# Hybrid decoder step: the per-layer embedding projection is placed among the last down slabs, and the final stage uses the pools of the second feed-forward block

## The chip, the cores and the metric

The kernel runs on one core of one Trainium2 chip. Its metric is the time of one execution in device microseconds (us). A core has TensorE (PE; loads of its stationary operand are listed apart as PEld), VectorE (DVE), ScalarE (ACT), GpSimd (POOL) and a queue engine (SP) that issues nearly all transfers. Each engine works through its own list of instructions in order; semaphores make one wait for another.

## The reference, cut to what matters

One layer on 544 tokens (512 of a new sequence, 8 times 4 of running ones), width 1024:

```python
x = x + 0.5 * _swiglu(_rmsnorm(x, n_f1), w_f1u, w_f1d)
m, ... = _mixer(_rmsnorm(x, n_mix), ...)               # SSD heads and HGRN2 heads
x = x + m
x = x + 0.5 * _swiglu(_rmsnorm(x, n_f2), w_f2u, w_f2d) # d_ff 2816
gate = sigmoid(_rmsnorm(x, n_ple) @ w_ple_gate)        # 1024 x 1024
e = _rmsnorm(p @ w_ple_proj, ple_post)                 # p: 544 x 256
x = x + gate * e
y = _rmsnorm(x, norm_final)
```

What matters here: `e` depends on the input `p` alone, not on `x`; `gate` needs the finished `x`.

## The kernel before

Everything is kept transposed: a tile is 128 features (partitions) by 544 tokens, and `x` is eight such tiles, `xs[0]` to `xs[7]`, parts of one buffer `xb`. fp32 products are made of three fp32r products: every operand is split into a high part (a rounded copy, made on ACT) and a low part (the rest, made on DVE), and hi·hi, hi·lo and lo·hi are summed in PSUM. `mm6` (line 229) is that for one 128x128 weight block and one tile: six matmuls of 272 columns. `slab` (line 133) loads eight weight blocks into a raw buffer `wraw`, of which there are two, and splits them into `whi` and `wlo`, of which there are three each. The PSUM pool `big` has two buffers; the down slabs, the embedding projection and the first gate products share it.

The stages around the change, in order:

- The second feed-forward block, `ffn` (line 235), with pool `f2`. Its up part runs in 18 periods in an order that is written out by hand (`pin` ties the instructions of each engine into a chain). The last group of six hidden tiles is multiplied by the down weights at its end: eight slabs, one for each `m`, 36 matmuls each, and after each one DVE adds the sum to `xs[m]` (line 643, in the trace `xb` at L72). There the chain is off (`pinned[0] = False`), and the framework's scheduler sets the order of each engine.
- The final stage, pool `f3` (line 1246). It loads `p` (`pt`), splits it into `pth` and `ptl`, and computes `e` in eight groups (PSUM `ps_e`, 12 matmuls each, copied to SBUF by ACT at line 1269). `rms_split` splits the scaled `x` (`xwh` on ACT, `xwl` on DVE), and `rms_two` squares `x` on ACT and sums the squares into two accumulators, one on POOL and one on DVE. `gslab` loads and splits the gate weights (`gh`, `gl`). The gate products follow in two halves of 272 tokens, eight groups of 24 matmuls in each (PSUM `ps_pg` and `ps_s`, line 1344).
- A root mean square is made by `inv_rms2` (line 179): each accumulator is multiplied by a column of ones in five one-column products (PSUM `ps_s`; each is two passes in the trace), the root and the reciprocal are taken, and the result is spread by products with the identity. It is done for `x` (result `r`) and for `e` (`eacc`, which then scales the eight `e` tiles on DVE).

Of the kernel before, what the change touches and what calls it, by code (L numbers as in the profile page):

```python
# [9 lines left out]
F32 = mybir.dt.float32  # L10
# [7 lines left out]
P = 128  # L18
T = 544
# [29 lines left out]
def body(ctx, tc, xT, pT, hconv, hssm, hhg, vecs, csts, w1u, w1d, w_in, w_dt, w_o, w2u, w2d, w_pg, w_pp,  # L49
# [21 lines left out]
    def stt(out, a, s, b, op0, op1):  # L71
        pin(V.scalar_tensor_tensor(out=out, in0=a, scalar=s, in1=b, op0=op0, op1=op1))  # L72
# [161 lines left out]

    def ffn(xs, nname, wu, wd, fp, ht, acc=None, load=None, side=iter(())):
        pinned[0] = True
# [403 lines left out]
        for m in range(KD):  # L640
            t = ts_[m] if m < 2 else last_slab(m)
            part(t, range(n - 1, n) if m < 2 else range(n))
            stt(h2(xs[m]), t[0][:, :, :HN], 0.5, h2(xs[m]), ALU.mult, ALU.add)

    x_sp = dram.tile([KD, P, T], F32, name="x_sp")
# [94 lines left out]
    with tc.tile_pool(name="ma", bufs=20, reuse_waits="tile") as ap:  # L740
# [499 lines left out]

        with tc.tile_pool(name="f2", bufs=1, reuse_waits="tile") as fp:
            ffn(xs, "n_f2", w2u, w2d, fp, ring, acc2, side=ssm_updates(
                fp, ring, lambda: xp2.tile([P, 512], F32R, name="xst", tag="sqa", bufs=1)))


    with tc.tile_pool(name="f3", bufs=34, reuse_waits="tile") as fp:
        def hslot(nm, dt=F32):
            return fp.tile([P, T], dt, name=nm, tag="h")

        def eslot(nm, dt=F32):  # L1250
            return fp.tile([P, T], dt, name=nm, tag="e", bufs=12)

        ph, es = [], []
        wpp = [slab(w_pp[i]) for i in range(2)]
        for k in range(2):
            t = eslot("pt")
            nc.sync.dma_start(t, pT[k])
            hi, lo = eslot("pth", F32R), eslot("ptl", F32R)
            A.copy(hi, t)
            tt(lo, t, f32(hi), ALU.subtract)  # L1260
            ph.append((hi, lo))
        for m in range(KD):
            hi, lo = wpp[m // 4]
            ps = big.tile([P, 2, 512], F32, name="ps_e", tag="big")
            for k in range(2):
                i = 2 * (m % 4) + k
                mm6(ps, hi[:, i], lo[:, i], ph[k][0], ph[k][1], k == 0, k == 1)
            e = eslot("e")
            A.copy(h2(e), ps[:, :, :HN])
            es.append(e)  # L1270
        xw = rms_split(xs, "n_ple")
        acc_x = rms_two(xs, fp)
        eacc = fp.tile([P, T], F32, name="eacc", bufs=1)

        def e_scale():
            ea = rms_two(es, fp)
            yield
            inv_rms(eacc, ea, 1024)
            for m in range(KD):
                stt(es[m], es[m], vc("ple_post", m), eacc, ALU.mult, ALU.mult)  # L1280
            yield

        eg = e_scale()
        wg = []

        def gslab(m):
            hi = [hslot("gh", F32R) for _ in range(2)]
            lo = [hslot("gl", F32R) for _ in range(2)]
            raw = wp.tile([P, 8, P], F32, name="wraw", tag="wraw", bufs=2)
            nc.sync.dma_start(raw, w_pg[m])  # L1290
            for i in range(2):
                rv = raw[:, 4 * i:4 * i + 4].rearrange("p a b -> p (a b)")
                A.copy(hi[i][:, :512], rv)
                tt(lo[i][:, :512], rv, f32(hi[i][:, :512]), ALU.subtract)
            wg.append((hi, lo))

        gslab(0)
        gslab(1)

        def final(hf, acc, sq):  # L1300
# [4 lines left out]
            for c, o in enumerate(cks):  # L1305
                PE.matmul(pq[:, c:c + 1], acc[:, o:o + P], ones[:, 0:1], start=True, stop=True)
            ra = fp.tile([P, 8], F32, name="ra", bufs=2)
            V.tensor_copy(ra[:, 0:3], pq[:, 0:3])
# [6 lines left out]
            for c, o in enumerate(cks):  # L1315
                a = 2 * P - o if c == 2 else 0
                PE.matmul(pr[:, o + a:o + P], ra[:, c:c + 1].to_broadcast([P, P]), cs("ident")[:, a:], start=True,
                          stop=True)
            rs = hslot("rs")[:, :HN]
            A.copy(rs, pr[:, :HN])  # L1320
# [10 lines left out]
        for hf in range(2):  # L1331
# [3 lines left out]
            for m in range(KD):  # L1335
# [10 lines left out]
                if hf == 0 and m == 1:  # L1346
                    r = rms_r(acc_x)
                if hf == 0 and m in (2, 4):
# [6 lines left out]
                for i, ps in pend:  # L1355
                    t = fp.tile([P, HN], F32, name="gt", tag="ft", bufs=4)
                    tt(t, ps[:, :HN], r[:, sl], ALU.mult)
                    act(t, t, AF.Sigmoid)
                    if hf == 1 and i == KD - 1:
                        tc.keep_in_program_order(A.preload_act_table(AF.Sqrt))  # L1360
                    tt(t, t, es[i][:, sl], ALU.mult)
                    tt(xs[i][:, sl], xs[i][:, sl], t, ALU.add)
                    sq = xqa[:, sl] if i == 0 else fp.tile([P, HN], F32, name="xq", tag="xq", bufs=2)
                    act(sq, xs[i][:, sl], AF.Square)
                    act(xs[i][:, sl], xs[i][:, sl], AF.Copy, scale=vc("n_fin", i))
                    if acc is None:
                        acc = sq
                    elif i < KD - 1:
                        tt(acc, acc, sq, ALU.add)
                pend = []  # L1370
            fin = final(hf, acc, sq)
        for _ in fin:
            pass


# [98 lines left out]
```

## Time and profile before

| | |
|---|---|
| median of 3 runs | 1417.15 us (1417.12 to 1419.89) |
| the profiled execution | 1418.97 us, of which the span of the engines is 1417.2 us |
| TensorE busy | 1384.7 us, 98% of the span |
| VectorE / ScalarE / GpSimd busy | 1000.6 / 684.3 / 268.8 us |
| mean granted TensorE clock | 0.984 of full speed |
| TensorE in the chain that ended last | 92% |

A row of the timeline gives the start, the duration, the engine, the line, the operation with output and inputs, a count, and in brackets how long the engine had sat idle and for whom. A matmul of 272 columns is listed at some 288 ns, but matmuls overlap, so that the next begins 125 ns later; a busy TensorE can still be one at half its clock, and the column PEclk of a stretch tells which. The last 94 us of the span, after the last down slab, are the final stage.

### The profile page before, as it was taken

Reading aid. Unit: us, or ns where it says so; the run is one execution under the profiler, and the core shown is the slowest. Engines: PE = TensorE matmul, PEld = TensorE weight load, DVE = VectorE, ACT = ScalarE, POOL = GpSimd, SP = SyncE. Lnnn points to the kernel's source line nnn. Section 1 sums busy time; section 2 is a strip of 40 time slices with the busy share of each in tenths; the row PEclk is TensorE's granted clock in tenths of the full one; section 3 lists DMA queues with packets and bytes.
Section 4 is the critical chain, followed back from the end, with each engine's and each line's share of the span. In section 5 each row is a group of like instructions: output and inputs, shape, how many; then the busy total and the mean of one; then the engine's idle time right before and its main releaser. Section 6 shows DMA issues by size and latency. Waiting matters only on the chain.

```text
span 1417.2 us, 27123 instructions
## 1 busy us (share of the span) xinstructions
PE 1384.7 (98%) x11069; PEld 1342.9 (95%) x11069; DVE 1000.6 (71%) x1603; ACT 684.3 (48%) x1232; POOL 268.8 (19%) x245
## 2 busy tenths in 40 slices
PE   7999999999999999999999999999899999999997
PEld 7999999999999999999999799999899999999896
DVE  6696666666568887777776577566877777776465
ACT  6544444443444365555553375455444444443655
POOL 0133332232111100000001021101333333320200
PEclk9999999999999999999999999999999999999898
DMA  6133233332432422222222445551344443334311
GB/s 228 43 93 105 90 90 94 100 95 73 149 111 77 139 93 93 93 93 93 93 100 72 140 152 172 187 170 46 107 120 125 128 137 120 119 101 116 105 45 64
DMA packets 67901, 154.99 MB, mean 109 GB/s; under 512 B 8576, under 2 KB 15872, under 8 KB 67776
## 3 DMA queue, kind: packets, MB, share of 16 engines
q1 hardware_dynamic: 66192, 150.65, 33.7%
q10 hardware_dynamic: 1584, 2.61, 0.5%
q8 instruction: 87, 1.43, 0.4%
q14 instruction: 38, 0.31, 0.1%
HBM read 138.70 MB, written 14.52 MB: 108 GB/s over the span
## 4 chain that ended last, share of the span: by engine, by line
PE 92%; DVE 4%; ACT 2%; issue 1%; DMA 0%; SPq 0%; DVEq 0%; ACTq 0%
PE ps_in L84 22%; PE ps_s L84 19%; PE ps_dn L84 19%; PE ps_ed L84 10%; PE ps_wo L84 6%; PE ps_up L84 4%; PE ps_s L1344 3%; PE ps_e L84 1%; PE ps_s L946 1%; PE ps_s L943 1%; PE ps_pg L1344 1%; DVE wlo L69 1%; DVE raw L69 1%; ACT whi L81 1%; PE ps_s L1056 1%
## 5 line engine op out<-in xcount | busy, mean ns | idle before, releaser
L81 ACT CAST whi<-wraw 128x1024 fp32r<-128x1024 f32 (+2 forms) x140 | 132.2, 950 | 200.5 <-PE ps_in L84 88.8
L69 DVE TENSOR_TENSOR wlo<-wraw,whi 128x1024 fp32r<-128x1024 f32 (+2 forms) x140 | 156.9, 1125 | 82.5 <-ACT whi L81 78.5
L84 PE MATMUL ps_in<-xwh,whi 128*128 128x272 f32 x832 | 183.6, 297 | 0.0
L84 PE MATMUL ps_in<-xwh,wlo 128*128 128x272 f32 x832 | 175.5, 291 | 0.0
L84 PE MATMUL ps_in<-xwl,whi 128*128 128x272 f32 x832 | 173.6, 289 | 0.0
L84 PEld LDWEIGHTS ps_in<-xwh,whi 128*128 128x128 f32 x832 | 132.4, 188 | 8.5 <-issue 8.2
L81 ACT COPY s<-ps_s 128x272 f32<-128x272 f32 x108 | 41.5, 384 | 195.5 <-PE ps_s L84 195.5
L84 PEld LDWEIGHTS ps_in<-xwh,wlo 128*128 128x128 f32 x832 | 130.7, 189 | 2.9 <-issue 2.9
L84 PEld LDWEIGHTS ps_in<-xwl,whi 128*128 128x128 f32 x832 | 131.1, 189 | 1.5 <-issue 1.5
L84 PE MATMUL ps_dn<-hl,dh 128*128 128x272 f32 x512 | 106.0, 288 | 2.5 <-DVE hl L69 2.5
L84 PE MATMUL ps_dn<-hh,dh 128*128 128x272 f32 x512 | 106.2, 289 | 0.0
L84 PE MATMUL ps_dn<-hh,dl 128*128 128x272 f32 x512 | 105.8, 288 | 0.0
L69 POOL TENSOR_TENSOR wraw<-r,r 128x512 f32<-128x512 f32 x36 | 48.7, 1353 | 263.4 <-DVE r L69 263.4
L84 PE MATMUL ps_s<-bx,w3h 128*128 128x272 f32 x576 | 85.2, 291 | 3.5 <-ACT s L81 3.5
L84 PEld LDWEIGHTS ps_dn<-hl,dh 128*128 128x128 f32 x512 | 80.5, 188 | 3.0 <-DVE hl L69 3.0
L84 PEld LDWEIGHTS ps_s<-bx,w3h 128*128 128x128 f32 x576 | 77.6, 191 | 3.9 <-ACT s L81 3.9
L84 PEld LDWEIGHTS ps_dn<-hh,dl 128*128 128x128 f32 x512 | 80.3, 188 | 0.2 <-DVE dl L69 0.2
L84 PEld LDWEIGHTS ps_dn<-hh,dh 128*128 128x128 f32 x512 | 80.4, 189 | 0.0
L69 POOL TENSOR_TENSOR g<-g,r 128x544 f32<-128x544 f32 x36 | 64.7, 1797 | 57.3 <-ACT g L89 56.0
L89 ACT ACT_TABLE_LOAD x55 | 70.6, 1283 | 4.4 <-DVE g L69 3.2
L69 DVE TENSOR_TENSOR w3l<-r,w3h 128x1024 fp32r<-128x1024 f32 x38 | 46.8, 1230 | 34.7 <-ACT w3h L81 34.7
L69 POOL TENSOR_TENSOR r<-r,wraw 128x512 f32<-128x512 f32 x36 | 49.2, 1366 | 103.4 <-DMA wraw<-in_w2u 54.8
(385 smaller groups left out, 3579.0 us busy)
## 6 DMA issues: line engine op xcount, KB each, us to landing
wraw<-in_w_in SPq DMA_DIRECT2D x52, 512.0 KB, 3.3
r<-in_w1u SPq DMA_DIRECT2D x22, 512.0 KB, 4.6
r<-in_w2u SPq DMA_DIRECT2D x22, 512.0 KB, 4.8
dr<-in_w1d SPq DMA_DIRECT2D x32, 256.0 KB, 3.3
h<-in_hssm SPq DMA_DIRECT2D x32, 256.0 KB, 4.1
wraw<-in_w_o SPq DMA_DIRECT2D x16, 512.0 KB, 4.2
dr<-in_w2d SPq DMA_DIRECT2D x32, 256.0 KB, 3.6
r<-in_w1u SPq DMA_DIRECT2D x18, 256.0 KB, 3.1
```

The source lines that it names most:

```text
L69: pin((eng or V).tensor_tensor(out=out, in0=a, in1=b, op=op))
L81: pin(A.copy(out, a))
L84: pin(PE.matmul(out, w, x, **kw))
L89: ins = pin(A.activation(out=out, in_=in_, func=f, scale=scale, bias=bias, **kw))
L943: PE.matmul(py[64 * e:64 * e + 64, q * P:q * P + n], xdt[:n, 2 * q + e], E[:n, 2 * q + e, :n], start=True, stop=pi is None, tile_position= ...
L946: PE.matmul(py[:, q * P:q * P + n], yf[:, q * P:(q + 1) * P], cs("sel") if smpl else cs("ident"), start=False, stop=True)
L1056: PE.matmul(pat[32 * j:32 * j + 32, c * P:(c + 1) * P], cw[:, c * P + 32 * j:c * P + 32 * j + 32], qs, start=True, stop=True, tile_positio ...
L1344: PE.matmul(ps[:, :HN], w[k // 4][:, k % 4 * P:k % 4 * P + P], xw[k][x][:, sl], start=k == 0 and n == 0, stop=k == KD - 1 and n == 2)
```

## The change

`ffn` gets an argument `done_m`, a function that it calls after each of the eight last down slabs. The final stage no longer opens a pool of its own. In the function `after_m` that is handed over, slab by slab:

- after every slab, `xs[m]` is split (`xwh`, `xwl`) and squared, and the square is added on DVE to one accumulator (`sqa`) instead of two;
- after slab 2, `p` is loaded and split and the first half of the projection weights is loaded; after slab 3, four of the eight `e` groups are computed; after slabs 5 and 6 the second half and the gate slabs 0 and 1 are loaded; after slab 6 come two `e` groups, after slab 7 the last two. Each `e` tile is squared and summed on DVE into one accumulator (`ea`).

The tiles take slots of the feed-forward block: `xw2`, `g`, `s53`, `s12`, `r1` to `r3`, `w3h`, `w3l`, `w5h`, `w5l`, `dh`, `dl`, and the ring of 544-wide tiles. The diff, without the lines that only rename a slot in the gate loop:

```diff
@@ -232,7 +232,7 @@
                 mm(ps, (lo if n == 2 else hi)[:, o + k], (xl if n == 1 else xh)[:, k % 2],
                    start=start and k == 0 and n == 0, stop=k == 3 and n == 2, skip_group_check=not start)
 
-    def ffn(xs, nname, wu, wd, fp, ht, acc=None, load=None, side=iter(())):
+    def ffn(xs, nname, wu, wd, fp, ht, acc=None, load=None, side=iter(()), done_m=None):
         pinned[0] = True
         chain.clear()
         X = {}
@@ -641,6 +641,8 @@
             t = ts_[m] if m < 2 else last_slab(m)
             part(t, range(n - 1, n) if m < 2 else range(n))
             stt(h2(xs[m]), t[0][:, :, :HN], 0.5, h2(xs[m]), ALU.mult, ALU.add)
+            if done_m:
+                done_m(m)
 
     x_sp = dram.tile([KD, P, T], F32, name="x_sp")
     acs_d = dram.tile([5, 16, P], F32, name="acs_d")
@@ -1238,64 +1240,95 @@
             acc2 = rms_sq(xs, xp2, 6, tmp=xp)
 
 
-        with tc.tile_pool(name="f2", bufs=1, reuse_waits="tile") as fp:
-            ffn(xs, "n_f2", w2u, w2d, fp, ring, acc2, side=ssm_updates(
-                fp, ring, lambda: xp2.tile([P, 512], F32R, name="xst", tag="sqa", bufs=1)))
-
-
-    with tc.tile_pool(name="f3", bufs=34, reuse_waits="tile") as fp:
-        def hslot(nm, dt=F32):
-            return fp.tile([P, T], dt, name=nm, tag="h")
-
-        def eslot(nm, dt=F32):
-            return fp.tile([P, T], dt, name=nm, tag="e", bufs=12)
-
-        ph, es = [], []
-        wpp = [slab(w_pp[i]) for i in range(2)]
-        for k in range(2):
-            t = eslot("pt")
-            nc.sync.dma_start(t, pT[k])
-            hi, lo = eslot("pth", F32R), eslot("ptl", F32R)
-            A.copy(hi, t)
-            tt(lo, t, f32(hi), ALU.subtract)
-            ph.append((hi, lo))
-        for m in range(KD):
-            hi, lo = wpp[m // 4]
-            ps = big.tile([P, 2, 512], F32, name="ps_e", tag="big")
+        end = ExitStack()
+        fp = end.enter_context(tc.tile_pool(name="f2", bufs=1, reuse_waits="tile"))
+
+        def et(nm, dt=F32):
+            return fp.tile([P, T], dt, name=nm, tag="xw2", bufs=12)
+
+        def ft(tag, nm, bufs, dt=F32):
+            return fp.tile([P, T], dt, name=nm, tag=tag, bufs=bufs)
+
+        ph, es, xw, ea, wpp = [], [], [], {}, []
+
+        def square(key, src, tags, home):
+            if key not in ea:
+                ea[key] = home()
+                act(ea[key], src, AF.Square)
+            else:
+                sq = ft(*tags)
+                act(sq, src, AF.Square)
+                tt(ea[key], ea[key], sq, ALU.add)
+
+        def e_load():
             for k in range(2):
-                i = 2 * (m % 4) + k
-                mm6(ps, hi[:, i], lo[:, i], ph[k][0], ph[k][1], k == 0, k == 1)
-            e = eslot("e")
-            A.copy(h2(e), ps[:, :, :HN])
-            es.append(e)
-        xw = rms_split(xs, "n_ple")
-        acc_x = rms_two(xs, fp)
-        eacc = fp.tile([P, T], F32, name="eacc", bufs=1)
+                t = ring("pt")
+                nc.sync.dma_start(t, pT[k])
+                hi, lo = et("pth", F32R), et("ptl", F32R)
+                A.copy(hi, t)
+                tt(lo, t, f32(hi), ALU.subtract)
+                ph.append((hi, lo))
+
+        def e_part(ms):
+            for m in ms:
+                hi, lo = wpp[m // 4]
+                ps = big.tile([P, 2, 512], F32, name="ps_e", tag="big")
+                for k in range(2):
+                    i = 2 * (m % 4) + k
+                    mm6(ps, hi[:, i], lo[:, i], ph[k][0], ph[k][1], k == 0, k == 1)
+                e = et("e")
+                A.copy(h2(e), ps[:, :, :HN])
+                es.append(e)
+                square("e", e, ("s53", "esq", 2), lambda: ft("s12", "ea", 1))
+
+        def after_m(m):
+            xw.append(split(xs[m], vc("n_ple", m)))
+            square("x", xs[m], ("g", "sq", 2), lambda: xp2.tile([P, T], F32, name="sqa", tag="sqa", bufs=1))
+            if m == 2:
+                e_load()
+                wpp.append(slab(w_pp[0]))
+            elif m == 3:
+                e_part(range(4))
+            elif m == 5:
+                wpp.append(slab(w_pp[1]))
+                gslab(0)
+            elif m == 6:
+                e_part((4, 5))
+                gslab(1)
+            elif m == 7:
+                e_part((6, 7))
 
         def e_scale():
-            ea = rms_two(es, fp)
             yield
-            inv_rms(eacc, ea, 1024)
+            eacc = ft("g", "eacc", 2)
+            inv_rms(eacc, [ea["e"]], 1024)
             for m in range(KD):
                 stt(es[m], es[m], vc("ple_post", m), eacc, ALU.mult, ALU.mult)
             yield
 
-        eg = e_scale()
         wg = []
 
         def gslab(m):
-            hi = [hslot("gh", F32R) for _ in range(2)]
-            lo = [hslot("gl", F32R) for _ in range(2)]
+            if m in (0, 4, 5, 6, 7):
+                hi, lo = ([ring(n, F32R)[:, :512] for _ in range(2)] for n in ("gh", "gl"))
+            else:
+                f = lambda n, w: fp.tile([P, w, P], F32R, name="gw", tag=n, bufs=1).rearrange("p a b -> p (a b)")
+                if m == 3:
+                    hi, lo = f("r3", 8), (f("w5h", 4), f("w5l", 4))
+                else:
+                    hi, lo = [f(n, 8) for n in (("w3h", "w3l") if m == 1 else ("r1", "r2"))]
+                hi, lo = [t if isinstance(t, tuple) else (t[:, :512], t[:, 512:]) for t in (hi, lo)]
             raw = wp.tile([P, 8, P], F32, name="wraw", tag="wraw", bufs=2)
             nc.sync.dma_start(raw, w_pg[m])
             for i in range(2):
                 rv = raw[:, 4 * i:4 * i + 4].rearrange("p a b -> p (a b)")
-                A.copy(hi[i][:, :512], rv)
-                tt(lo[i][:, :512], rv, f32(hi[i][:, :512]), ALU.subtract)
+                A.copy(hi[i], rv)
+                tt(lo[i], rv, f32(hi[i]), ALU.subtract)
             wg.append((hi, lo))
 
-        gslab(0)
-        gslab(1)
+        ffn(xs, "n_f2", w2u, w2d, fp, ring, acc2, side=ssm_updates(
+            fp, ring, lambda: xp2.tile([P, 512], F32R, name="xst", tag="sqa", bufs=1)), done_m=after_m)
+        eg = e_scale()
 
         def final(hf, acc, sq):
             sl = slice(hf * HN, (hf + 1) * HN)
...
                 if hf == 0 and m == 1:
-                    r = rms_r(acc_x)
+                    r = rms_r([ea["x"]])
```

The order of ScalarE's instructions, where the down slabs end and `p` is cast. Before, from the split of `xs[6]` on:

```order
L89 ACTIVATE xwh_15724<-xb_9826,vec_67 128x544
L89 ACTIVATE sq_15732<-xb_9826 128x544
L89 ACTIVATE sq_15734<-xb_9826 128x544
L89 ACTIVATE xwh_15728<-xb_9826,vec_67 128x544
L89 ACTIVATE sq_15737<-xb_9826 128x544
L89 ACTIVATE sq_15740<-xb_9826 128x544
L1259 CAST pth_15570<-pt_15568 128x544
```

Now, at the second of the eight down slabs (`hh_15232` is the last hidden tile, `whi_15301` and `whi_15370` are the weights of down slabs 2 and 3, `whi_15364` the projection weights):

```order
L81 CAST whi_15301<-wraw_15300 128x768
L81 CAST hh_15232<-g_15172 128x544
L1268 CAST pth_15353<-pt_15351 128x544
L81 CAST whi_15364<-wraw_15363 128x1024
L1268 CAST pth_15359<-pt_15357 128x544
L81 CAST whi_15370<-wraw_15369 128x768
L89 ACTIVATE xwh_15280<-xb_9826,vec_67 128x544
```

The first cast of `p` has moved from behind the split of the last `xs[m]` and two squares to a place ahead of the third down slab.

VectorE at the same place. Before, after the last state update (`h0_15175`); `ps_dn_15157` and `ps_dn_15217` are the sums of down slabs 0 and 1, whose PSUM buffers the slabs 2 and 3 take over:

```order
L69 TENSOR_TENSOR h0_15175<-h0_15175,ps_s_15269 128x512
L72 SCALAR_TENSOR_TENSOR xb_9826<-ps_dn_15157,xb_9826 128x544
L69 TENSOR_TENSOR wlo_15333<-wraw_15331,whi_15332 128x768
L72 SCALAR_TENSOR_TENSOR xb_9826<-ps_dn_15217,xb_9826 128x544
L69 TENSOR_TENSOR wlo_15377<-wraw_15375,whi_15376 128x768
```

Now, up to the low part of the weights of down slab 3 (`wlo_15371`; before it was `wlo_15333`):

```order
L69 TENSOR_TENSOR h0_15175<-h0_15175,ps_s_15269 128x512
L69 TENSOR_TENSOR ptl_15354<-pt_15351,pth_15353 128x544
L72 SCALAR_TENSOR_TENSOR xb_9826<-ps_dn_15157,xb_9826 128x544
L72 SCALAR_TENSOR_TENSOR xb_9826<-ps_dn_15217,xb_9826 128x544
L69 TENSOR_TENSOR ptl_15360<-pt_15357,pth_15359 128x544
L69 TENSOR_TENSOR wlo_15365<-wraw_15363,whi_15364 128x1024
L72 SCALAR_TENSOR_TENSOR xwl_15281<-xb_9826,vec_67,xwh_15280 128x544
L69 TENSOR_TENSOR sqa_15284<-sqa_15284,sq_15297 128x544
L72 SCALAR_TENSOR_TENSOR xwl_15294<-xb_9826,vec_67,xwh_15293 128x544
L69 TENSOR_TENSOR wlo_15371<-wraw_15369,whi_15370 128x768
```

One instruction now stands ahead of the first `xb`, and six of the final stage stand ahead of the low part of slab 3's weights.

VectorE later, around down slab 6 (`ps_dn_15615`); `gw_15697` and `gw_15861` are the low parts of gate slabs 1 and 2, `wlo_15706` that of down slab 7:

```order
L69 TENSOR_TENSOR gw_15697<-wraw_15698,gw_15696 128x512 x2
L72 SCALAR_TENSOR_TENSOR xb_9826<-ps_dn_15548,xb_9826 128x544
L72 SCALAR_TENSOR_TENSOR xwl_15587<-xb_9826,vec_67,xwh_15586 128x544
L69 TENSOR_TENSOR sqa_15284<-sqa_15284,sq_15590 128x544
L69 TENSOR_TENSOR wlo_15706<-wraw_15704,whi_15705 128x768
L69 TENSOR_TENSOR gw_15861<-wraw_15862,gw_15860 128x512
L72 SCALAR_TENSOR_TENSOR xb_9826<-ps_dn_15615,xb_9826 128x544
L69 TENSOR_TENSOR gw_15861<-wraw_15862,gw_15860 128x512
L72 SCALAR_TENSOR_TENSOR xwl_15654<-xb_9826,vec_67,xwh_15653 128x544
```

The addition of down slab 6 to `xb`, which frees the PSUM buffer of the sixth `e` group, stands behind the first half of gate slab 2, and so behind that slab's transfer.

## Rows read from the trace of the kernel before

**Rows 1.** Chain of waits, 1290 to 1350 us: start, duration, what.
```profile
1295.53 27.25 PE ps_dn L84 x216
...
1322.80 0.74 DVE xb L72
...
1325.31 0.64 ACT pth L1259
...
1346.86 3.25 PE ps_pg L1344 x26
```

**Rows 2.** Instructions on tile ps_e: min/median/max ns, first and last start.
```profile
L84 PE MATMUL ps_e<-pth,whi x32: 285/288/593, 1326.0 to 1346.1; 128*128 128x272 f32 x32
```

**Rows 3.** Timeline of TensorE, rows from the whole span.
```profile
400.51 1.20 PE L84 MATMUL ps_s<-cst,ra 128*128 128x128 f32 x10
...
829.02 1.17 PE L84 MATMUL ps_s<-ones,ysq 128*128 128x1 f32 x10
...
842.25 1.28 PE L84 MATMUL ps_s<-ones,ysq 128*128 128x1 f32 x10 [0.78 <-DVE ysq L69]
...
1325.99 1.05 PE L84 MATMUL ps_e<-pth,whi 128*128 128x272 f32 x3 [3.23 <-ACT pth L1259]
...
1352.70 0.75 PE L84 MATMUL ps_s<-cst,ra 128*128 128x128 f32 x6
...
1362.37 2.29 PE L84 MATMUL ps_s<-ones,sq 128*128 128x1 f32 x20
...
1365.24 1.94 PE L84 MATMUL ps_s<-cst,ra 128*128 128x128 f32 x10 [0.58 <-DVE ra L180]
```

**Rows 4.** Stretches: length, busy PE, PEld, DVE, ACT, POOL, PEclk, DMA share, GB/s.
```profile
829.00:830.00 1.00, 1.00 (x12) 1.00 (x10) 1.00 (x3) 0.98 (x3) 0.00 (x0) 1.00 0.06 16
...
844.00:845.00 1.00, 1.00 (x6) 1.00 (x6) 1.00 (x2) 0.99 (x5) 0.00 (x0) 0.50 0.56 158
...
1290.00:1322.00 32.00, 31.93 (x255) 31.67 (x255) 20.29 (x27) 13.32 (x18) 1.01 (x1) 1.00 0.37 116
...
1326.00:1338.20 12.20, 12.20 (x53) 11.91 (x54) 6.59 (x9) 7.52 (x13) 2.05 (x2) 0.50 0.14 44
...
1368.00:1369.00 1.00, 1.00 (x7) 1.00 (x6) 1.00 (x2) 0.00 (x0) 0.00 (x0) 0.50 0.00 0
```

**Rows 5.** Timeline of VectorE, 1294 to 1377 us.
```profile
1295.41 0.96 DVE L69 TENSOR_TENSOR wlo<-wraw,whi 128x768 fp32r<-128x768 f32 x1
1296.29 0.72 DVE L72 SCALAR_TENSOR_TENSOR xb<-ps_dn,xb 128x544 f32<-128x544 f32 x1
...
1297.79 1.48 DVE L72 SCALAR_TENSOR_TENSOR xwl<-xb,vec,xwh 128x544 fp32r<-128x544 f32 x2
...
1314.69 1.23 DVE L69 TENSOR_TENSOR wlo<-wraw,whi 128x1024 fp32r<-128x1024 f32 x1 [0.15 <-ACT whi L81]
...
1330.89 0.72 DVE L69 TENSOR_TENSOR ptl<-pt,pth 128x544 fp32r<-128x544 f32 x1
...
1367.65 5.66 DVE L72 SCALAR_TENSOR_TENSOR e<-e,vec,eacc 128x544 f32<-128x544 f32 x8 [2.47 <-ACT eacc L81]
...
1376.40 0.43 DVE L69 TENSOR_TENSOR gt<-ps_s,r 128x272 f32<-128x272 f32 x1
```

**Rows 6.** Timeline of the weight loads where down slab 2 begins.
```profile
1295.53 0.30 PEld L84 LDWEIGHTS ps_dn<-hh,whi 128*128 128x128 f32 x2 [0.29 <-DVE xb L72]
```

**Rows 7.** Instructions that write or read sq: min/median/max ns.
```profile
L69 DVE TENSOR_TENSOR sq<-sq x17: 718/725/1656, 24.8 to 1348.5; 128x544 f32<-128x544 f32 x17
...
L69 POOL TENSOR_TENSOR sq<-sq x14: 1341/1366/2182, 369.0 to 1345.6; 128x544 f32<-128x544 f32 x14
```

**Rows 8.** Transfers of the last 150 us, and of in_w_pg.
```profile
wraw<-in_w2d SPq DMA_DIRECT2D x8, 384.0 KB, 3.4
...
DMA to landing us min/median/max: 3.1/3.2/4.4
```

**Rows 9.** Instructions on tile wraw, 1300 to 1365 us: min/median/max ns.
```profile
L1293 ACT CAST gh<-wraw x16: 603/616/622, 1328.0 to 1361.7; 128x512 fp32r<-128x512 f32 x16
```

More of the change, by code (lines that the diff above doesn't have):

```diff
@@ L1306, in final @@
                 PE.matmul(pq[:, c:c + 1], acc[:, o:o + P], ones[:, 0:1], start=True, stop=True)
-            ra = fp.tile([P, 8], F32, name="ra", bufs=2)
+            ra = wp.tile([P, 8], F32, name="ra", tag="ra", bufs=2)
             V.tensor_copy(ra[:, 0:3], pq[:, 0:3])
@@ L1318, in final @@
                           stop=True)
-            rs = hslot("rs")[:, :HN]
+            rs = ft("g", "rs", 2)[:, :HN]
             A.copy(rs, pr[:, :HN])
@@ L1355, in body @@
                 for i, ps in pend:
-                    t = fp.tile([P, HN], F32, name="gt", tag="ft", bufs=4)
+                    t = fp.tile([P, 4, P], F32, name="gt", tag=("dh", "dl")[i % 2], bufs=2).rearrange("p a b -> p (a b)")[:, :HN]
                     tt(t, ps[:, :HN], r[:, sl], ALU.mult)
@@ L1362, in body @@
                     tt(xs[i][:, sl], xs[i][:, sl], t, ALU.add)
-                    sq = xqa[:, sl] if i == 0 else fp.tile([P, HN], F32, name="xq", tag="xq", bufs=2)
+                    sq = xqa[:, sl] if i == 0 else ft("s53", "xq", 2)[:, :HN]
                     act(sq, xs[i][:, sl], AF.Square)
@@ L1373, in body @@
             pass
+        end.close()
 _INS = ["xT", "pT", "hconv", "hssm", "hhg", "vecs", "csts", "w1u", "w1d", "w_in", "w_dt", "w_o", "w2u",
```

## The prediction

> **What bounds the kernel now.** The page's table of busy engines came first: TensorE is busy for 98% of the span and stands for 92% of the chain of waits. So the time is the sum of the matmuls, unless TensorE waits or runs at less than its full clock, and I looked for those places from the last down slabs on, where the diff begins. The chain of waits shows the seam [rows 1]: 216 down matmuls run without a break from 1295.53 to 1322.78 us, then the chain leaves TensorE for DVE and ACT until `p` is cast, and the gate products begin only at 1346.86. TensorE's own timeline gives the wait: 3.23 us for the first `pth` [rows 3]. The stretches give the rest: from 1326.0 to 1338.2 TensorE is busy all the time but at a granted clock of 0.50, 1.2 GHz, while it had 1.00, 2.4 GHz, up to 1322 [rows 4]. What it did before the fall was to wait, and what it did in the slow stretch was partly 20 one-column passes for the mean square of `x`. There is a second such stretch, still at 0.50 at 1368, after the 20 one-column passes for `e` and a wait of 0.58 us [rows 3, 4]. The list of DMA waits held nothing for TensorE here.
>
> **The change part by part.** Up to down slab 1 all engines have the same order; the terms begin there.
>
> 1. *The seam goes.* From 1322.78 to 1346.86 are 24.08 us [rows 1]. The work in it at full clock: 96 matmuls on `ps_e` (three forms of 32 [rows 2]), at 27.25 / 216 = 0.126 us each [rows 1], 12.1 us; 20 one-column passes, 2.29 us; four passes of 128 columns at 0.75 / 6 us, 0.5 us [rows 3]. That is 14.9 us, so 9.2 us were lost: 3.2 us of waiting, the rest half clock. In the changed order `p` is cast before down slab 2, the last two `e` groups (24 matmuls, 3.0 us) stand behind down slab 7, and the last `xb` and the split of `xs[7]` (0.72 and 0.78 us on DVE [rows 5], and one pass of ACT over a tile of that size, as for `pth`, 0.64 [rows 1]) are done beside them, and the gate products come to `xs[7]` last. What is late next is then the psum copy of the `e` groups (term 3). Gain 9.2 us; its lower bound is the 3.2 us of waiting alone, should the slow clock stay for another reason.
>
> 2. *One accumulator instead of two.* Both mean squares take 10 one-column passes instead of 20. Twenty took 2.29 us, ten took 1.17 us [rows 3]: 1.1 us each, 2.2 us. The 14 additions that this puts on DVE, eight of them more than before (six went to POOL), are 0.72 us each where POOL is quiet [rows 7], 10.1 us beside some 40 us of matmuls, in which DVE was busy 20.3 of 32 us [rows 4]: hidden, but queued ahead of things TensorE waits for (term 3). If that cover were gone, 5.8 us at most would come back. On these additions the Trainium skill (SBUF — State Buffer, Who interferes with whom) says that a DVE instruction with two inputs in SBUF shuts out a GpSimd instruction that reads SBUF, and the reverse. The trace agrees: the same addition took 725 ns as a rule and up to 1656 where POOL added too [rows 7]. With POOL idle the sum has 0.72 us for each; by 1.66 us it would have 0.9 us more in the wait for slab 3's weights.
>
> 3. *New waits in the down slabs.* Slab 2 takes over the PSUM buffer of slab 0, and TensorE already waits 0.29 us for DVE's `xb` there [rows 6]. One `ptl` (0.72 us, 0.64 to the next start [rows 5]) now stands ahead of it: 0.6 us more, slab 2 begins at 1296.1. Its 36 matmuls end at 1296.1 + 36 x 0.126 = 1300.6, and slab 3 needs its low weights after four more, at 1301.1. On DVE, from the first `xb` on, stand `xb` 0.72, `ptl` 0.72, `wlo` of the projection 1.23, `xwl` 0.78, an addition 0.72, `xwl` 0.78 and that `wlo` 0.96 [rows 5, 7]; less 0.08 us of overlap at each step (eight of 0.78 take 5.66 [rows 5]) it is done at 1301.4: 0.3 us of waiting. Before down slab 7 TensorE needs the PSUM buffer of the fifth `e` group, whose copy stands on ACT behind a split and a square of `xs[6]`: it is ready about when the sixth group ends, 0 to 0.4 us, and I take 0.4. The sixth `e` group needs `xb` of slab 6, which stands behind half of gate slab 2. That slab's load is issued about when slab 5 ends (T); landing 3.2 us [rows 8], cast 0.62 [rows 9], low half 0.96 x 512 / 768 = 0.64 [rows 5], issue and steps between some 0.4: T + 4.9, then `xb` to T + 5.6, needed at T + 36 x 0.126 + 12 x 0.126 = T + 6.0. So nothing, with 0.4 us to spare. Sum 1.3 us lost; the bounds are 0.3 us and, with all these transfers at the 4.4 us that one gate slab took [rows 8], 4 us.
>
> 4. *The second slow stretch* stays in the forecast. Ten passes (1.17 us) and a wait of some 0.6 us for root and reciprocal remain. The row nearest to that is at 842: a wait of 0.78 us and ten passes, after which the clock fell to 0.50 at 844; ten passes at 829 without a wait left it at 1.00 [rows 3, 4]. Cost of the change 0; if it goes, up to 1.8 us are gained (the ten passes of 128 columns took 1.94 instead of 1.20 us [rows 3], and some 2 us of matmuls until 1369 took twice their time [rows 4]). About 0.65 us of that would turn into a wait, since DVE frees the next PSUM buffer only at 1376.83 [rows 5], 9.65 us after the last of those passes, and three gate groups at full clock take 9.0 us.
>
> The loads, casts and splits of the gate weights keep their number; they are made earlier, on queues that had room (ACT busy 13.3 of 32 us [rows 4]), and cost nothing unless they come late. Nothing changes in the last half of the gate or in the end.
>
> Sum: 9.2 + 2.2 - 1.3 = 10.1 us. The profiled execution took 1418.97 us (span 1417.2 us and 1.8 us around it), so it would take 1408.9 us; it lies 1.8 us above the median of the runs, 1417.15 us, from which I get 1407.1 us.
>
> **The rivals.**
>
> *The second fall goes too.* For it: half the passes, and the ones at 829 had no fall. Against it: the wait behind them stays, as at 842. It gives 1.2 us more: 1405.9 us.
>
> *Small waits add up and the clock falls in the down slabs.* If transfers land later than 3.2 us, the sixth `e` group waits (1.2 us if gate slab 2 alone takes 4.4 us), other waits grow, and TensorE works in short groups with pauses. One fall costs about 1.8 us, as in term 4. For it: the two raw buffers now carry three streams through one SP queue, and each load waits for DVE. Against it: the clock stayed at 1.00 with the 0.29 us wait [rows 4, 6]. Waits of 4 instead of 1.3 us, and one fall: 10.1 - 2.7 - 1.8 = 5.6 us of gain, 1411.5 us. The Trainium skill has a rule on the side of this rival (TensorE: Matmul & The Clock Gate, A second HAM failure mode: psum-queue depth-cycling): a TensorE that pauses briefly between groups as it goes round its PSUM banks can swing between its two clocks. The wait of 0.29 us, with the clock at 1.00 after it, does not bear it out; the fall at 844, after 0.78 us and the one-column passes, can be read its way.
>
> *Slower: the two raw buffers become the bound.* Between slab 2's weights and the start of slab 7, ten loads pass through the two `wraw` buffers, five each. A round is landing 3.4, a cast 0.62 x 768 / 512 = 0.93 and a low part 0.96 us [rows 5, 8, 9], 5.3 us; five rounds are 26.5 us, and end at 1322.6 even if they begin only with slab 2, at 1296.1. TensorE starts slab 7 at about 1296.1 + 5 x 4.54 + 6 x 1.51 = 1328. So each round may take 6.4 us before slab 7 is late at all, and at 8.8 us slab 7 is 12 us late and the time 2 us above before, 1419. For it: every load waits for a DVE instruction that stands in order behind others. Against it: the longest landing in the rows is 4.4 us, and DVE had 12 of 32 us free.
>
> *It doesn't do what it says.* If TensorE still met `pth` or the first projection weights late, or lost at the gate what it gains at the seam, the time stays at about 1417. The order on ACT speaks against it: the cast of `p` waits there for its transfer alone, with ACT idle.
>
> **How the numbers follow.** Forecast 1407.1 us: 0.47. Second fall gone: 0.25, 1405.9. Small waits and a fall: 0.20, 1409 to 1414. No change: 0.05. Slower: 0.03. The range goes from the sum with the second fall gone and the lower bound of the waits (10.1 + 1.2 + 1.0 = 12.3 us, 1404.8) to just beyond the price of the third case, 1412.0; what it leaves out is a part of the third case and the last two. A measurement of this kernel tells about 0.2% (2.8 us) from no change: faster by more, below 1414.3 us, 0.93; within it 0.04; slower 0.03.
>
> **What the changed profile would show.** Right: no wait of TensorE for `pth`; a granted clock of 1.00 from 1300 to the gate products, which begin near 1336; ones products in groups of ten passes; waits of `ps_dn` for `xb` under 1 us and for `wlo` of about 0.3 us; the `e` stretch near 1355 with a fall behind it. Wrong: a wait of over 1 us inside the down slabs with PEclk 0.50 behind it, TensorE waiting for a transfer of `w2d` or `w_pg`, or gate products that begin later than 1340.

## The result and the profile after

The changed kernel takes 1408.07 us (median of 6 runs, 1405.26 to 1411.82), the kernel before 1417.13 us (6 runs, 1413.29 to 1419.89): a ratio of 0.9939, 95% interval 0.9922 to 0.9956. A second series of 5 runs gave 1408.17 us, ratio 0.9932 (0.9918 to 0.9945). The forecast was 1407.1 us.

The profiled execution of the changed kernel took 1406.71 us, its span is 1404.9 us, against 1418.97 and 1417.2. Of these 12.3 us, 2.75 lie ahead of the change. The last state product on TensorE, up to which all engines have the same order, begins earlier by that (start, duration, then engine, line and operation; before first):

```profile
1293.57 0.39 PE L84 MATMUL ps_s<-xst,Bm 128*128 128x512 f32 x1
```

```profile
1290.82 0.39 PE L84 MATMUL ps_s<-xst,Bm 128*128 128x512 f32 x1
```

The last section says more on that. What the change does is counted from this product on: 9.6 us less (123.63 and 114.08 us to the end), where the sum in the prediction was 10.1; between the medians it is 9.1 us.

First the chain of waits of the changed kernel from slab 2 to the gate products, start, duration and what; it answers to [rows 1]:

```profile
1293.27 5.26 PE ps_dn L84 x40
1298.56 4.28 PE ps_dn L84 x32
1302.83 4.54 PE ps_e L84 x36
...
1313.06 4.67 DMA wraw<-in_w_pg
1317.75 0.63 ACT gw L1325
1318.41 1.31 DVE gw L69 x2
1319.73 3.12 DMA wraw<-in_w_pg
1322.87 0.63 ACT gw L1325
1323.53 0.69 DVE gw L69
1324.22 0.65 DVE xb L72
...
1326.74 4.78 PE ps_dn L84 x36
1331.52 3.02 PE ps_e L84 x24
1334.54 6.00 PE ps_pg L1377 x48
```

The seam is gone: the gate products begin at 1334.54, 41.3 us after slab 2 begins (51.3 before). The six slabs and eight `e` groups in between are 27.25 + 12.1 = 39.3 us, so 1.9 us of waiting are left. For one part of it the chain leaves TensorE and follows two transfers of gate weights. TensorE's own timeline has these waits, and those at `e` [rows 3 and 6 show them before]:

```profile
1293.27 0.52 PE L84 MATMUL ps_dn<-hh,whi 128*128 128x272 f32 x2 [0.55 <-DVE xb L72]
...
1324.91 0.52 PE L84 MATMUL ps_e<-pth,whi 128*128 128x272 f32 x2 [0.95 <-DVE xb L72]
...
1351.58 1.17 PE L84 MATMUL ps_s<-ones,ea 128*128 128x1 f32 x10
...
1353.33 1.30 PE L84 MATMUL ps_s<-cst,ra 128*128 128x128 f32 x10 [0.58 <-DVE ra L180]
...
1364.47 0.39 PE L1377 MATMUL ps_s<-xwh,gh 128*128 128x272 f32 x1 [0.77 <-DVE gt L69]
```

And the stretches, columns as in [rows 4], the first two with the same bounds as there, the third behind the passes for `e`:

```profile
1290.00:1322.00 32.00, 31.42 (x247) 30.94 (x247) 23.51 (x34) 20.20 (x32) 0.00 (x0) 1.00 0.42 131
1326.00:1338.20 12.20, 12.15 (x97) 11.93 (x96) 10.37 (x17) 9.95 (x19) 0.00 (x0) 1.00 0.47 142
1353.30:1357.30 4.00, 3.97 (x33) 3.97 (x34) 2.07 (x3) 0.67 (x2) 0.00 (x0) 1.00 0.01 4
```

The granted clock is 1.00 in all three: neither of the two slow stretches of before is there. The second one was expected to stay.

### The profile page after: what moved, and what is told of

It reads as the page before. It is cut to its first block, busy times and chain, and to the rows that moved or that the text cites. A ratio compares the mean times of both kernels' runs of the same rounds, so it can differ in the third digit from the quotient of the medians.

```text
span 1404.9 us, 27066 instructions
## 1 busy us (share of the span) xinstructions
PE 1372.5 (98%) x11049; PEld 1330.0 (95%) x11049; DVE 1003.5 (71%) x1611; ACT 683.5 (49%) x1232; POOL 259.1 (18%) x239
## 4 chain that ended last, share of the span: by engine, by line
PE 90%; DVE 5%; ACT 2%; DMA 1%; issue 1%; SPq 0%; DVEq 0%; ACTq 0%
PE ps_in L84 22%; PE ps_s L84 19%; PE ps_dn L84 18%; PE ps_ed L84 10%; PE ps_wo L84 6%; PE ps_up L84 4%; PE ps_s L1377 2%; DVE wlo L69 1%; PE ps_s L948 1%; PE ps_s L945 1%; PE ps_pg L1377 1%; DVE raw L69 1%; ACT whi L81 1%; PE ps_s L925 1%; PE ps_s L1058 1%
## 5 line engine op out<-in xcount | busy, mean ns | idle before, releaser
L81 ACT COPY s<-ps_s 128x272 f32<-128x272 f32 x108 | 41.3, 383 | 192.4 <-PE ps_s L84 192.3
```

Source lines behind the costliest of these rows:

```text
L81: pin(A.copy(out, a))
```

## The experiments

The total of one run moves by several us with the part ahead of slab 2. So each kernel is measured twice: by its time, and, in its trace, by the stretch from the start of slab 2 to the end of the last gate product, both read from the chain of waits (the chain of `before_one_acc` leaves TensorE where the gate begins, so there the end of the last `e` product is taken). In the three kernels with two traces that stretch repeats within 0.15 us. It leaves out that slab 2 begins 2.45 instead of 1.96 us after the last state product in the changed kernel, since `ptl` stands ahead of the first `xb`; so it does in all others with an early `p` except `combo` and `combo2`. Each ratio is to runs of before in the same series.

| kernel | us (runs) | ratio to before, 95% | slab 2 to gate | slab 2 to last gate product |
|---|---|---|---|---|
| before, first / again | 1417.13 (6) / 1416.90 (10) | 1 / 1.0003 (0.9993 to 1.0013) | 51.3 / 51.4 | 108.1 / 108.3 |
| changed, first / again | 1408.07 (6) / 1408.17 (5) | 0.9939 / 0.9932 | 41.3 / 41.1 | 97.9 / 97.8 |
| `p_early_e_last` | 1406.54 (6) | 0.9926 (0.9906 to 0.9946) | 40.7 | 96.3 |
| `p_late_e_last` | 1410.77 (6) | 0.9952 (0.9933 to 0.9971) | 46.1 | 101.2 |
| `two_acc` | 1409.38 (6) | 0.9943 (0.9924 to 0.9961) | 40.1 | 100.8 |
| `xb_first` | 1407.20 (6) | 0.9923 (0.9902 to 0.9944) | 40.3 | 97.2 |
| `before_one_acc` | 1414.06 (12) | 0.9977 (0.9964 to 0.9990) | 47.3 | 105.0 |
| `e_with_x` | 1404.89 (6) | 0.9916 (0.9893 to 0.9939) | 40.7 | 95.2 |
| `combo` | 1404.65 (4) | 0.9910 (0.9885 to 0.9935) | 41.2 | 96.0 |
| `combo2`, first / again | 1405.34 (6) / 1401.66 (4) | 0.9913 / 0.9890 | 40.5 / 40.5 | 94.0 / 94.0 |

**`p_early_e_last`: only `p` early.**

```diff
             if m == 2:
                 e_load()
-                wpp.append(slab(w_pp[0]))
-            elif m == 3:
-                e_part(range(4))
...
             elif m == 7:
-                e_part((6, 7))
+                wpp.extend(slab(w_pp[i]) for i in range(2))
+                e_part(range(8))
+                gslab(0)
+                gslab(1)
```

> The changed kernel, but only the load and the split of p stay among the down slabs (called after slab 2); both halves of the projection weights, all eight e groups and the gate slabs 0 and 1 are called after slab 7, as before. Theory (the seam was lost because p came late, and the place of the e groups gives nothing): no wait for pth, clock 1.00 from slab 2 to the gate products, which begin some 40 to 42 us after slab 2 begins (41.3 in the changed kernel); time within 1.5 us of the changed kernel, rather below it, as the waits of 0.3 us for wlo of slab 3 and 0.95 us before the sixth e group go. Rival (the e groups must lie among the slabs, since at the end their PSUM copies on ACT and their sums on DVE come thick): waits of ps_e or ps_pg of 2 us and more, and a time 3 to 5 us above the changed kernel.

Its chain of waits, the same places as above:

```profile
1296.58 27.44 PE ps_dn L84 x216
1324.02 10.73 PE ps_e L84 x84
...
1337.24 6.11 PE ps_pg L1371 x48
```

The 216 down matmuls run without a break as in [rows 1], and the `e` groups follow them without one. From the end of slab 7 to the gate are 13.2 us instead of 24.08. So the seam goes with no `e` group among the slabs; how much of that is the early `p` alone, the next run tells. With the groups among the slabs the stretch to the last gate product is 1.6 us longer, by the waits at slab 3's weights, the sixth group and slab 7. The times, 1406.54 and some 1408.1 us, don't tell this apart, the traces do.

**`p_late_e_last`: `p` behind the gate loads again.** As the last, but after slab 7 the gate slabs 0 and 1 are called first, then `e_load()` and the `e` groups, and `e_load` has this:

```diff
-                nc.sync.dma_start(t, pT[k])
+                after(nc.sync.dma_start(t, pT[k]), gdma[-1])
```

> The kernel p_early_e_last with one thing more: the two loads of p are issued behind the load of gate slab 1, where they stood in the kernel before (1320.85 us there). Single accumulators and the pools of the change stay. Theory (p late causes the wait, the wait causes the slow clock): TensorE waits 2.5 to 3.5 us after slab 7, the granted clock falls to 0.50 during the wait and stays there for 8 to 13 us, and the time is 6 to 9 us above p_early_e_last, near 1415. Rival (the 20 one-column passes held the clock down, the wait alone costs little): the clock falls for about 3.4 us as at 844 or not at all, and the time is 3 to 5 us above p_early_e_last.

TensorE's timeline behind slab 7, and the stretches:

```profile
1325.55 1.27 PE L84 MATMUL ps_s<-ones,sqa 128*128 128x1 f32 x10 [3.07 <-DVE sqa L69]
1326.68 0.74 PE L84 MATMUL ps_e<-pth,whi 128*128 128x272 f32 x4
```

```profile
1325.50:1327.50 2.00, 1.96 (x15) 1.78 (x16) 1.83 (x3) 1.97 (x4) 0.00 (x0) 1.00 0.05 21
1327.80:1331.00 3.20, 3.20 (x16) 3.20 (x16) 2.09 (x4) 1.51 (x3) 0.00 (x0) 0.50 0.45 159
1331.50:1335.00 3.50, 3.50 (x29) 3.33 (x28) 1.28 (x2) 3.50 (x7) 0.00 (x0) 1.00 0.34 132
```

The wait is back, and after it the clock falls, but for 3.4 us only, not 13. Here the ten passes for `x` stand first in TensorE's order and wait for their last sum on DVE; the cast of `pth` (from 1325.52, 0.64 us) ends while they run. So the fall follows a wait and ten passes, and this run doesn't tell the two apart. The time is 4.2 us above `p_early_e_last`: the rival's numbers. So a late `p` with ten passes costs about half of what the seam cost before.

**`before_one_acc`: before, ten passes instead of twenty.**

```diff
-            if k in (0, 4):
+            if k == 0:
                 accs.append(sq)
             else:
-                tt(accs[-1], accs[-1], sq, ALU.add, eng=G if k < 4 else V)
+                tt(accs[-1], accs[-1], sq, ALU.add)
```

> The kernel before with one accumulator for each mean square, summed on DVE; nothing else is changed, so p still comes late. Theory W (the wait of 3.2 us starts the slow clock, and 20 one-column passes inside the slow stretch keep it there): the wait stays at 3 to 3.5 us, the slow stretch shrinks from 13.4 us to between 3.4 and 7 us, worth 3 to 5 us, and ten passes fewer at x and at e are worth 2.2 us: 5 to 7 us below before, about 1411. Rival (the slow stretch hangs on the wait alone): it stays at 13 us, and the time is 2 us below before. Second rival (the early p and the new pools are what made p_late_e_last faster): 0 to 2 us below before, with additions on DVE that come late ahead of the passes for x.

```profile
1325.37 1.28 PE L84 MATMUL ps_e<-pth,whi 128*128 128x272 f32 x4 [3.23 <-ACT pth L1259]
1330.20 0.82 PE L84 MATMUL ps_e<-ptl,whi 128*128 128x272 f32 x2 [0.30 <-DVE ptl L69]
1331.65 1.17 PE L84 MATMUL ps_s<-ones,sq 128*128 128x1 f32 x10
...
1361.42 2.11 PE L84 MATMUL ps_s<-cst,ra 128*128 128x128 f32 x10 [2.25 <-DVE ra L180]
```

```profile
1324.50:1330.90 6.40, 5.21 (x19) 4.47 (x20) 6.09 (x11) 5.11 (x10) 0.00 (x0) 0.50 0.00 0
1331.50:1335.00 3.50, 3.50 (x31) 3.50 (x30) 1.36 (x3) 3.47 (x6) 0.00 (x0) 1.00 0.57 167
1362.00:1365.00 3.00, 3.00 (x15) 3.00 (x15) 1.00 (x2) 0.67 (x2) 0.00 (x0) 0.50 0.00 0
```

With the same wait of 3.23 us the clock falls before any one-column pass, as it did in before. Read in stretches of 1 us, the slow stretch lasts some 6.8 us instead of 13.6 (13.7 in the second trace of before), and the passes for `x` now come only behind it. So the length is as theory W has it, and the rival that expected 13 us is out. But no pass stands inside the slow stretch any more, so whether their number or their place made it shorter isn't shown. The gain is 3.0 us, between the 5 to 7 of the theory and the 2 of its rival: the additions, now all on DVE, stand ahead of `ptl` (TensorE is busy for 5.21 of 6.40 us), and at `e` the root stands on ACT behind casts that wait for gate weights, 2.25 instead of 0.58 us.

**`two_acc`: the change with twenty passes.**

```diff
-            if key not in ea:
-                ea[key] = home()
+            n = cnt[key] = cnt.get(key, -1) + 1
+            if n in (0, 4):
+                if n:
+                    key = key + "2"
+                ea[key] = home() if not n else ring("acc2")
...
+                key = key + "2" * (n > 4)
```

> The changed kernel with two accumulators for each mean square, as before, so 20 one-column passes instead of 10 for x and for e. Theory (term 2, and the second fall went because half the passes went): 1.1 us more for each of the two, and the clock at 0.50 for some 3.4 us after the passes for e, about 1.7 us, of which 0.77 us is given back as the wait for a PSUM buffer goes: 3.0 us above the changed kernel. Rival (the passes are not what made the second fall): the clock stays at 1.00 behind the e passes, and the time is 2.2 us above the changed kernel. A third outcome (what the passes save is lost in the wait for DVE's scaling of e anyway): under 1.5 us.

Its chain of waits, TensorE's timeline behind the passes for `e`, and the stretches:

```profile
1322.07 3.10 PE ps_e L84 x24
...
1333.02 6.05 PE ps_pg L1381 x48
1339.07 1.90 PE ps_s L84 x18
...
1351.20 2.14 PE ps_s L84 x20
```

```profile
1354.21 2.35 PE L84 MATMUL ps_s<-cst,ra 128*128 128x128 f32 x10 [0.89 <-DVE ra L180]
```

```profile
1339.00:1341.00 2.00, 2.00 (x20) 2.00 (x19) 0.69 (x1) 1.72 (x2) 0.00 (x0) 1.00 0.58 215
1354.00:1360.50 6.50, 6.29 (x28) 6.29 (x29) 3.62 (x7) 0.67 (x2) 0.00 (x0) 0.50 0.01 3
```

The 18 passes for `x` in one piece from 1339.07, with no wait beside them, leave the clock at 1.00. The 20 for `e`, with a wait of 0.89 us, are followed by 6.8 us at 0.50. So the rival, a clock of 1.00, is out. The stretch to the last gate product grows by 2.9 us, and that it is so near the forecast of 3.0 is luck. Behind the start of the gate it grows by 4.1 us (56.6 to 60.7), with a slow stretch twice as long as forecast; 1.1 us are given back ahead of it, because DVE's order is another here (`xb` of slab 6 stands ahead of the low parts of gate slab 2) and the sixth `e` group doesn't wait. The time is about 1.3 us longer, which is within the spread of either kernel and by itself would also fit the third outcome.

**`xb_first`: one order on DVE.**

```diff
-                tt(lo[i], rv, f32(hi[i]), ALU.subtract)
+                ins = V.tensor_tensor(out=lo[i], in0=rv, in1=f32(hi[i]), op=ALU.subtract)
+                if m in (1, 2):
+                    after(ins, xbs[-3 if m == 1 else -2])
```

The part for gate slab 1 (`m == 1`) asks for an order that the changed kernel has already: there these low parts begin at 1318.41 us, after the addition of slab 4 at 1313.42.

> The changed kernel with one order fixed on DVE: the low parts of gate slab 2 follow the addition of down slab 6 to xb instead of standing ahead of it. Theory (the sixth e group waits only because xb stands behind that transfer): the wait of 0.95 us goes to under 0.2, nothing takes its place, and the time is 0.9 us below the changed kernel. Rival (the next thing is as late: the copy of the fifth e group ahead of slab 7, 0.37 us now, or the gate weights): the wait before slab 7 grows by as much, and the time is the same within 0.3 us.

TensorE's list of waits (total, times, longest) has only one wait for `xb` now, the one at slab 2; then the start of the gate in the chain of waits:

```profile
PE ps_dn L84 <- DVE xb L645: 0.6, 1, 0.6
```

```profile
1332.82 6.26 PE ps_pg L1381 x48
```

The wait at the sixth group is gone, and the gate begins 0.9 us sooner (40.3 us after slab 2); at the last gate product 0.7 us are left, or 0.6 against the second trace of the changed kernel. `two_acc`, which has this order too, has no wait there either. The mechanism is shown; the time, 1407.20 us, agrees and can't tell 0.9 us.

**`e_with_x`: the root of `e` right behind that of `x`.**

```diff
                     r = rms_r([ea["x"]])
-                if hf == 0 and m in (2, 4):
-                    next(eg)
+                    eacc = e_inv()
...
-                if hf == 0 and m < 4:
+                if hf == 0 and m < 1:
                     continue
...
                     tt(t, ps[:, :HN], r[:, sl], ALU.mult)
+                    if hf == 0:
+                        stt(es[i], es[i], vc("ple_post", i), eacc, ALU.mult, ALU.mult)
```

> The changed kernel with the root mean square of e taken right behind that of x, after the second gate group instead of the fifth, and the eight products that scale e spread over DVE's work on the gate, each ahead of its use; the gate groups 0 to 3 are no longer held back until the fifth. Theory (with e early, the wait of 0.58 us for the root of e and that of 0.77 us for a PSUM buffer behind 5.66 us of scaling are left only by the order): both go to under 0.2 us, the time is 1.3 us below the changed kernel. Rival (DVE, which now has scale, gate and squares at once, becomes late for the PSUM buffers): TensorE waits for gt 1 us and more in other places, no gain.

```profile
1334.65 5.98 PE ps_pg L1373 x48
...
1343.86 2.12 PE ps_s L84 x20
...
1351.09 18.02 PE ps_s L1373 x144
```

Both waits are gone: behind the sixth `e` group TensorE's list of waits has none before the final root, and the chain stays on TensorE, where in the changed kernel it follows DVE's scaling of `e`. The stretch is 95.2 instead of 97.9 us. Of these 2.7 us 0.5 is a shorter wait at the sixth group in this trace, and 1.35 are the two waits; where the other 0.9 lies was not followed up. The time is 1404.89 us.

**`combo` and `combo2`.** `combo` is the change with `e_with_x`, `xb_first`, `ptl` behind the first `xb`, and `slab(w_pp[0])` called after slab 3; `combo2` is `p_early_e_last` with `e_with_x` and `ptl` behind the first `xb`.

> The changed kernel (e groups among the slabs) with everything: e_with_x, xb_first, the low part of p behind the first xb, and the first projection weights called after slab 3 instead of slab 2, so that they stand behind the weights of down slab 3. Theory: the waits before slab 2, at the weights of slab 3, before the sixth e group, at the root of e and for gt (0.55, 0.3, 0.95, 0.58 and 0.77 us) all fall below 0.3 us; from the start of slab 2 to the end 2.5 to 3 us less than 111.6 us. Rival (the two raw buffers bring one of them back, since the projection weights are now loaded later): a wait of 1 us or more before the first e groups or at slab 4, and no gain over e_with_x.

> p_early_e_last (only p early, all e groups behind slab 7) with the order of e_with_x, and with the low part of p behind the addition of down slab 0 to xb on DVE. Theory (the groups among the slabs give nothing, and each wait left over is one of order): waits of under 0.3 us before slab 2 (0.55 in the changed kernel), none at e, none for gt; from the start of slab 2 to the end 1.9 to 2.5 us less than the changed kernel's 111.6 us. Rival (e groups at the end leave e's mean square late, so that the passes for e wait): 1 us of waiting at the passes for e, no gain over p_early_e_last.

`combo` gains nothing over `e_with_x`, as its rival had it, though no wait reaches the rival's 1 us. The wait before slab 2 goes, but there are waits of 0.35 us at the third `e` group and 0.53 us at the sixth. From the start of slab 2 its stretch is 0.8 us longer than that of `e_with_x`, and as slab 2 begins 0.5 us sooner, 0.3 us are lost in all. For `combo2` the list of TensorE's waits is empty from slab 2 to the last gate product; its chain of waits:

```profile
1292.88 27.24 PE ps_dn L84 x216
1320.13 10.75 PE ps_e L84 x84
...
1333.38 6.11 PE ps_pg L1369 x48
1339.49 2.12 PE ps_s L84 x20
```

It was run again beside the changed kernel, with before once more:

> combo2 once more, on the same chip as the changed kernel. Theory (it is shorter by 3.9 us between the start of slab 2 and the last gate product, and its median was raised by falls of the clock earlier in the program that have nothing to do with the edit): again 93.5 to 94.5 us in that stretch, and 3 to 4 us below the changed kernel's time. Rival (its order makes the earlier falls likelier): a time within 2 us of the changed kernel, with a long fall near 990.

> The changed kernel once more, as the measure for combo2_again, and to see a second time whether the clock falls behind the ten passes for e. Theory (ten passes and 0.58 us of waiting don't lower the clock): 1.00 behind them; from the start of slab 2 to the last gate product 97 to 98.5 us as before; 1406 to 1409 us. Rival (the fall there is chance): 0.50 for some 3.4 us, and the wait for gt is gone.

> The kernel before once more, for the two slow stretches. Theory: again the wait of 3.2 us at the seam with 0.50 for 10 to 14 us, and 0.50 behind the 20 passes for e. Rival (their lengths are chance): a seam stretch under 7 us, or none behind the passes for e.

The lines above are of the second trace of `combo2`. Its stretch repeats (94.0), 3.8 us under the change: 1.6 us of that are `p_early_e_last`, and 2.2 the order of `e_with_x`. From the start of slab 2 to the end it is 4.4 and 4.1 us less in the two traces, about twice the 1.9 to 2.5 that were expected. Its time in that series is 1401.66 us against 1408.17 of the changed kernel, which here had the long fall near 990 that the rival laid on `combo2`. By the stretch it is the shortest version; its times don't settle that, since in the first series 1405.34 us lay within the spread of `e_with_x` and `combo`. The changed kernel shows no fall behind the passes for `e` a second time; before has both slow stretches a second time.

## Why the prediction was right, and where it was not

1. *The seam* (9.2 us): right. In `p_early_e_last`, where the seam can be read by itself, it went from 24.08 to 13.2 us, 10.9 us less; the terms for it are 9.2, the 1.1 us of the ten passes and 0.5 us of four spreading passes that moved behind the gate's start. What the prediction did not separate is how the 9.2 us hang together: the 3.2 us wait is `p`'s, the rest is a slow stretch that comes with the wait and lasts nearly 14 us with 20 passes inside it, and 3.4 or 6.8 us in the two kernels with a wait and ten. Where the passes are ten, the early `p` is worth 4.9 us (101.2 to 96.3 at the last gate product), of which the later slab 2 takes 0.5 back; the times differ by 4.2. It does not need the `e` groups among the slabs.

2. *One accumulator* (2.2 us): right in size. The passes for `e` in the chain of waits: 1.02 instead of 2.14 us. Each addition took 716 to 724 ns with POOL idle from 1285 to 1377 us, as the sum had it. The price for a cover that is gone, which the prediction named, was seen in `before_one_acc`.

3. *New waits* (1.3 us): the mechanism right, one size wrong. Slab 2 begins 0.5 us later (0.6 was the forecast), and slab 3's weights and slab 7 cost some 0.3 us each, as forecast or less. The sixth `e` group was to have 0.4 us to spare and waited 0.95. The step that failed is "that slab's load is issued about when slab 5 ends": it was issued at 1319.73, some 2 us after that, since its raw buffer was free only when DVE had split gate slab 1, and that slab's transfer had taken 4.67 us [rows 8 give 3.2 as the middle and 4.4 as the longest]. Together 2.4 us (0.5 and the 1.9 above) instead of 1.3.

4. *The second slow stretch* (0): wrong. It went, a rival with a chance of 0.25. The step that failed is to take the row at 842 as the nearest. The changed kernel has the same wait and the same ten passes there, in two traces, and the clock fell in one of them:

```profile
841.09 1.28 PE L84 MATMUL ps_s<-ones,ysq 128*128 128x1 f32 x10 [0.77 <-DVE ysq L69]
...
842.00:846.00 4.00, 4.00 (x35) 4.00 (x35) 3.34 (x6) 3.06 (x6) 0.00 (x0) 1.00 0.24 70
```

```profile
843.88 1.28 PE L84 MATMUL ps_s<-ones,ysq 128*128 128x1 f32 x10 [0.77 <-DVE ysq L69]
...
847.00:849.00 2.00, 2.00 (x10) 2.00 (x10) 1.22 (x1) 0.86 (x2) 0.00 (x0) 0.50 0.07 19
```

One trace gives such a fall as if it were a property of the place. Over all thirteen traces the order here is the same and the wait 0.76 to 0.78 us, and the clock fell in four. Behind the passes for `e` the same wait of 0.58 us was followed by a fall in both traces with twenty passes (before) and in none of the five with ten (the changed kernel twice, `p_early_e_last`, `p_late_e_last`, `xb_first`). That speaks for the number of passes, as does `two_acc`, whose wait was longer; but ten passes with a wait of 2.25 us were followed by a fall too, in `before_one_acc`. What was given back is as worked out: at full clock TensorE reaches DVE's scaling early and waits 0.77 us for `gt` (0.65 in the prediction).

The misses of terms 3 and 4 go against each other: 1.1 us more of waiting, and 1.8 less 0.77 us from the clock, so that the corrected terms give 10.0 us, for 9.6 measured. That the sum came out so near is luck in these two terms. Of the rest 0.2 us is a longer end (13.7 us behind the last gate product instead of 13.5); some 0.3 us were not followed up. The other rivals did not come about: the raw buffers decided one wait, not the time. The Trainium skill's rule (TensorE: Matmul & The Clock Gate, A second HAM failure mode: psum-queue depth-cycling) made no difference here: with waits of 0.55 and 0.95 us between groups (the rows above) the clock stayed at 1.00 from 1290 to 1338.

## What to carry to other kernels

Ask of a slow stretch what started it and what keeps it up, apart: here an early load and cast removed the wait that it began with, what followed was shorter in the kernels with ten passes instead of twenty, and the work that was placed elsewhere brought waits of its own. A fall of the clock that one trace shows may be missing from the next: look at several before it is priced. A reduction whose input has become early should be taken early too, or its wait stays where the order left it. When runs differ by more than the edit is worth, compare a stretch of the trace that begins where the two orders part.

## What was not expected of the hardware

Falls of the clock in places where the order is the same come and go between executions. In the profiles of before they lie at 41, 86, 843, 990 and 1017 us in one and at 39, 988 and 1015 in the other; in the changed kernel at 38, 987 and 1014 in one, and at 40, 400, 846, 990 (7 us long) and 1020 in the other, where slab 2 begins 5.5 us later (1298.80). The six runs of the changed kernel show the same thing in their granted clocks: 0.995 at 1405.26 us, 0.988 at 1411.82. What decides whether such a place falls stays open; so does why a wait of 3.1 to 3.2 us was followed by 3.4 us at half clock in one kernel and by 6.8 in another.
